# Attention scores from stacked high and low halves in two passes, and the normalisation placed behind the next maximum, in a two-layer diffusion backbone

## The chip, the cores and the metric

The kernel runs on one core of one Trainium2 chip. The metric is the device time in microseconds (us). A core has five engines that run side by side and wait for one another by semaphores: TensorE (PE in the profile, its weight loads PEld), VectorE (DVE), ScalarE (ACT), GpSimd (POOL) and SyncE (SP, which issues most of the loads). Each engine works through its own instructions in the order in which the program emits them.

## What is computed

The reference is a two-layer backbone over 256 latent tokens and 256 context tokens of width 1024. Each layer projects the normalised tokens into a Fourier part, a pooling part, queries, keys, values and gates, mixes them in three branches, and then retrieves experts. The part that the change touches is the attention of one layer:

```python
q = apply_axial_rope(rmsnorm(q, q_norm[l]), ang_row, ang_col)     # 8 heads of 64
k = apply_axial_rope(rmsnorm(k, k_norm[l]), ang_row, ang_col)     # 2 key heads, 4 query heads each
kc = rmsnorm(kc, k_norm[l])
...
s = jnp.einsum('bqhgd,bkhd->bhgqk', q, k).astype(jnp.float32) * (HEAD_DIM ** -0.5)
p = jax.nn.softmax(s, axis=-1).astype(v.dtype)
return jnp.einsum('bhgqk,bkhd->bqhgd', p, v)
```

Latent queries (blocks 0 and 1 of 128 rows) read all 512 keys; context queries (blocks 2 and 3) read the 256 context keys, and only layer 0 has them.

## The kernel before

The order of the work on each engine is the order of the source (a manual schedule). Most large products are three passes over a high and a low half of both operands, kept in the type `fp32r` (helper `mm3`, lines 282 to 284; `split_to`, lines 287 and 289, makes the halves: ACT copies the high one, then DVE or POOL subtracts for the low one). The scores, the transposes against an identity and the products of probabilities and values are exact f32; the trace shows each such f32 call as two PE records ("x2").

`mixer(l, nrm, last)` runs once per layer. It makes `P` (queries and others, 4 blocks of 128 tokens in layer 0, `nq` = 2 in layer 1) and `KV` (keys in its first 128 columns). `rot` normalises and rotates them on DVE. Then come the Fourier and pooling branches, and then the attention:

- **The filler.** `fill()` computes gate projections (units `fills`) as a generator; one `next(filler)` emits six `fp32r` matmuls (L282 to L284, tile `gate`). Eight such steps are emitted ahead of the attention and 24 inside its loop. With the first steps of a unit POOL gets the two subtractions of 1024 columns for the next unit (L289).
- **The preparation (L645 to L653).** Four transposes of the keys (L647), copied to `kT` by ACT; then for each of four pairs of heads `nq` transposes of the queries (L652), copied to `qT`. A pair lies in one tile as two halves of 64 partitions. That is 20 transposes in layer 0 and 12 in layer 1. It is all emitted before the first score.
- **The loop (L710 to L721).** It has N items (head pair, query block, head of the pair): 32 in layer 0, of which 16 have 512 keys and 16 have 256, and 16 of 512 keys in layer 1, so 32 calls of 512 columns and 16 of 256 in all. Round n emits on each engine: `stage_norm(n-1)` (DVE: reciprocal L678, scaling L679), `stage_scores(n)` (PE: one score call L667 with 64 partitions; DVE: maximum L670, L671; ACT: exponential L673), the filler's share, `stage_T(n-2)` (PE transposes L685, ACT copy L687) and `stage_pv(n-3)` (PE products L700 into `ya`). In layer 0 the filler's 24 steps fall into 24 of the 32 rounds, in layer 1 every round has one or two.

Then the remaining gates, the projections of the branches, the output projection (`wout`) and the expert stage follow.

Of the kernel before, what the change touches and what calls it, by code (L numbers as in the profile page):

```python
# [10 lines left out]
F32 = mybir.dt.float32  # L11
F32R = mybir.dt.float32r
F16 = mybir.dt.float16
U32 = mybir.dt.uint32
AF = mybir.ActivationFunctionType
OP = mybir.AluOpType
# [44 lines left out]
def kernel(ctx_: ExitStack, tc: tile.TileContext, I, C, out):  # L61
    nc = tc.nc
# [29 lines left out]
    def b16(shape, dt=F32, name="b16"):  # L92
        return b16_p.tile(shape, dt, tag="b16", name=name)

    def b8(shape, dt=F32, name="b8"):
        return b8_p.tile(shape, dt, tag="b8", name=name)

    def b4(shape, dt=F32, name="b4"):
        return b4_p.tile(shape, dt, tag="b4", name=name)
# [4 lines left out]
    def psum(shape=(128, 512), dt=F32, name="ps"):  # L104
        return banks["ps"].tile(list(shape), dt, tag="ps", name=name)
# [4 lines left out]
    def dram(ap_src, off, dims):  # L110
        return bass.AP(tensor=ap_src.tensor, offset=ap_src.offset + off, ap=dims)
# [3 lines left out]
    ident = perm_p.tile([128, 128], F32, name="ident")  # L115
# [175 lines left out]
    def small(shape, dt=F32, name="small", bufs=None):  # L291
        return sm_p.tile(shape, dt, tag=name, name=name, bufs=bufs) if bufs else sm_p.tile(shape, dt, tag=name, name=name)
# [21 lines left out]
    p = psum()  # L314
# [76 lines left out]
    def ffn_rows(l):  # L391

        rows = small([40, 128], name="mrows", bufs=1)
        frows[l] = rows
        for s in range(2):
            for i, (g, o) in enumerate(((1, 1024), (2, 0))):
                r0 = 16 * s + 8 * i
                load(out=rows[r0:r0 + 8].rearrange("k (b j) -> k b j", b=4),
                     in_=md[l, g][s:s + 1, o:o + 1024].rearrange("a (b k j) -> (a k) b j", b=4, k=8))
        load(out=rows[32:40].rearrange("k (b j) -> k b j", b=4),  # L400
             in_=dram(I["norm_ffn"], l * D, [[32, 8], [256, 4], [1, 32]]))
# [78 lines left out]
    def mixer(l, nrm, last):  # L480
        nq = 2 if last else 4
        nt = nq * 128
        gains = b4([128, 640], name="gains")
        load(out=gains[:, :512].rearrange("p (h d) -> p h d", d=HD),
             in_=dram(I["q_norm"], l * HD, [[0, 128], [0, 8], [1, HD]]))
        load(out=gains[:, 512:].rearrange("p (h d) -> p h d", d=HD),
             in_=dram(I["k_norm"], l * HD, [[0, 128], [0, 2], [1, HD]]))
# [10 lines left out]
        P = b16([128, 4, 1024], name="P")  # L498
        KV = b4([128, 4, 256], name="KV")
# [59 lines left out]
                nc.vector.tensor_tensor(out=v, in0=v, in1=rope[:, b, 0:1, :].to_broadcast([128, nh, HD]), op=OP.mult)  # L559
                nc.vector.tensor_tensor(out=src, in0=src, in1=t, op=OP.add)  # L560

        kT = b4([128, 512], name="kT")
        qT = b8([128, 4, nt], name="qT")
        for b in range(4):
            rot(b, KV[:, b, :128], 8, 2)
            if b < nq:
# [14 lines left out]
        for s in range(nq // 2):  # L581
            for c in range(2):
                ps = psum()
                for k in range(2):
                    nc.tensor.matmul(ps, lhsT=P[:, 2 * s + k, c * 128:(c + 1) * 128], rhs=dft[:, k, :],
                                     start=k == 0, stop=k == 1)
                nc.scalar.activation(pt[:, s, c, :], ps, AF.Copy)
        for c in range(2):
            ps = psum()
            for s in range(nq // 2):  # L590
                for q in range(2):
                    nc.tensor.matmul(ps[:, s * 256:(s + 1) * 256], lhsT=bd[:, q, :],
                                     rhs=pt[:, s, c, q * 256:(q + 1) * 256], start=q == 0, stop=q == 1)
# [4 lines left out]
        for c in range(2):  # L598
            ps = psum()
            for s in range(nq // 2):  # L600
                for g in range(2):
                    ch = 256 + c * 128 + g * 64
                    for k in range(2):
                        nc.tensor.matmul(ps[64 * g:64 * g + 64, s * 256:(s + 1) * 256],
                                         lhsT=P[:, 2 * s + k, ch:ch + 64], rhs=band[:, 2 * c + g, k, :],
                                         start=k == 0, stop=k == 1)
            nc.scalar.activation(pp[:, c, :], ps[:, :nt], AF.Copy)
        S.presplit()
        for c in range(2):
            ps = psum()  # L610
            nc.tensor.matmul(ps[:, :nt], lhsT=pw[:, c, :], rhs=pp[:, c, :], start=True, stop=True)
            t = b4([128, nt], name="pt")
# [29 lines left out]
        filler = fill()  # L642
        for _ in range(8):
            next(filler)
        ps = psum()  # L645
        for b in range(4):
            nc.tensor.transpose(ps[:, b * 128:(b + 1) * 128], KV[:, b, :128], ident)  # L647
        nc.scalar.activation(kT, ps, AF.Copy)
        for j in range(4):
            ps = psum()  # L650
            for b in range(nq):
                nc.tensor.transpose(ps[:, b * 128:(b + 1) * 128], P[:, b, 512 + j * 128:640 + j * 128], ident)  # L652
            nc.scalar.activation(qT[:, j, :], ps[:, :nt], AF.Copy)  # L653

        items = [(hc, b, e) for hc in range(4) for b in range(nq) for e in range(2)]
        st = {}
# [2 lines left out]
        def stage_scores(n):  # L659
            hc, b, e = items[n]  # L660
            h = 2 * hc + e
            v, j = divmod(h, 4)
            kb = (0, 4) if b < 2 else (2, 4)
            nk = (kb[1] - kb[0]) * 128
            ps = psum()
            s = slice(64 * v, 64 * v + 64)
            nc.tensor.matmul(ps[:, :nk], lhsT=qT[s, j, b * 128:(b + 1) * 128], rhs=kT[s, kb[0] * 128:kb[1] * 128],  # L667
                             start=True, stop=True)
            mx = small([128, 3], name="mx", bufs=6)
            nc.vector.tensor_reduce(out=mx[:, 0:1], in_=ps[:, :nk], op=OP.max, axis=AX)  # L670
            nc.vector.tensor_scalar(mx[:, 0:1], mx[:, 0:1], -0.125, None, op0=OP.mult)  # L671
            pm = ring[:, n % 4, :]
            nc.scalar.activation(pm[:, :nk], ps[:, :nk], AF.Exp, bias=mx[:, 0:1], scale=0.125, accum_out=mx[:, 1:2])  # L673
            st[n] = (pm, mx, kb, nk)

        def stage_norm(n):
            pm, mx, kb, nk = st[n]
            nc.vector.reciprocal(out=mx[:, 2:3], in_=mx[:, 1:2])  # L678
            nc.vector.tensor_scalar(pm[:, :nk], pm[:, :nk], mx[:, 2:3], None, op0=OP.mult)  # L679

        def stage_T(n):
            pm, mx, kb, nk = st[n]
            ps = psum()
            for q in range(nk // 128):
                nc.tensor.transpose(ps[:, q * 128:(q + 1) * 128], pm[:, q * 128:(q + 1) * 128], ident)  # L685
            pT = ring[:, 4 + n % 4, :]
            nc.scalar.activation(pT[:, :nk], ps[:, :nk], AF.Copy)  # L687
            st[n] = (pT, kb)
# [3 lines left out]
        def stage_pv(n):  # L692
            hc, b, e = items[n]
            v = (2 * hc + e) // 4
            pT, kb = st.pop(n)
            if b == 0 and e == 0:
                ya[hc] = psum(name="ya")
            for q in range(kb[0], kb[1]):
                o = (q - kb[0]) * 128
                nc.tensor.matmul(ya[hc][64 * e:64 * e + 64, b * 128:(b + 1) * 128],  # L700
                                 lhsT=KV[:, q, 128 + 64 * v:192 + 64 * v], rhs=pT[:, o:o + 128],
                                 start=q == kb[0], stop=q == kb[1] - 1)
            if b == nq - 1 and e == 1:
                split_to(yh[:, 4 + hc, :], yl[:, 4 + hc, :], ya.pop(hc)[:, :nt])

        N = len(items)
        filled = 0
        if l:
            ffn_rows(l)
        for n in range(N + 3):  # L710
            if 0 <= n - 1 < N:
                stage_norm(n - 1)
            if n < N:
                stage_scores(n)
            while filled < min(24 * (n + 1) // N, 24):
                next(filler, None)
                filled += 1
            if 0 <= n - 2 < N:
                stage_T(n - 2)
            if n >= 3:  # L720
                stage_pv(n - 3)  # L721
# [9 lines left out]
        for n, u in enumerate(rest):  # L731
# [22 lines left out]
            for c in range(2):  # L754
                w = slice(c * 128, (c + 1) * 128)
                for i, (k0, k1) in enumerate(br):
                    ps = psum()
# [435 lines left out]
    for l in range(DEPTH):  # L1193
        last = l == DEPTH - 1
        nb = 2 if last else 4
        mg = mixer(l, nrm, last)
        ffn_cols(l)

        def keys():
            kT = b8([128, 16, 128], name="keysT")  # L1200
            for q in range(4):
                ps = psum()
                for a in range(4):
                    nc.tensor.transpose(ps[:, a * 128:(a + 1) * 128], kr[:, 4 * q + a, :], ident)
                nc.scalar.activation(kT[:, 4 * q:4 * q + 4, :], ps.rearrange("p (a n) -> p a n", a=4), AF.Copy)
            return kT

        X = b16([128, nb, D], name="X")
        for b in range(nb):
            if l == 0:  # L1210
                src = I["x"][0, b * 128:(b + 1) * 128, :] if b < 2 else I["ctx"][0, (b - 2) * 128:(b - 1) * 128, :]
            else:
                src = xs[b]
# [27 lines left out]
        if nb == 4:  # L1241
# [12 lines left out]
            kT = keys()  # L1254
# [6 lines left out]
        else:  # L1261
# [10 lines left out]
            kT = keys()  # L1272
# [68 lines left out]
```

## Time and profile before

| | |
|---|---|
| median of three runs | 3029.86 us (3025.63 to 3040.64) |
| the profiled execution | 3029.89 us |
| its span, first to last instruction | 3028.1 us |
| mean granted TensorE clock | 0.963 of full speed |
| busy: PE, PEld, DVE, ACT, POOL | 2761.7, 2414.4, 2151.0, 1290.1, 1243.0 us |

The busy times are sums over the whole span; a PE record's end is modelled, and records of matmuls overlap, so the distance from one start to the next tells what a matmul takes. The attention of layer 0 lies at about 135 to 241 us of the span, that of layer 1 at about 1968 to 2030 us.

### The profile page before, as it was taken

What the parts mean: (1) busy time and instruction counts of PE and PEld (TensorE: products, weight loads), DVE (VectorE), ACT (ScalarE), POOL (GpSimd) and SP (SyncE); (2) the same over time, 40 slices, a digit from 0 to 9 for tenths busy, and PEclk for the clock granted to TensorE, in tenths of its full rate; (3) what the DMA queues carried; (4) which work ended last, traced back from release to release, by engine and by line L of the source; (5) the groups of instructions that cost most, each with busy time, mean ns of one, the idle gap of its engine ahead of it and who ended that gap; (6) DMA issues with size and microseconds to landing.
All of it is one profiled execution on the core that took longest, in us unless ns stands there. A gap on an engine that the chain in (4) does not pass through costs nothing.

```text
span 3028.1 us, 42396 instructions
## 1 busy us (share of the span) xinstructions
PE 2761.7 (91%) x16484; PEld 2414.4 (80%) x16484; DVE 2151.0 (71%) x3292; ACT 1290.1 (43%) x1955; POOL 1243.0 (41%) x634
## 2 busy tenths in 40 slices
PE   6999998999898888999998889799887998899999
PEld 4767786798888777987776777679887988888887
DVE  3444253599999999577776877646797889466666
ACT  3443222233334666332332223454544777544443
POOL 0110002234357898455665555020578767620000
PEclk8999999999999999999999999899999999999999
DMA  6215655768887797989999888426778899987874
GB/s 226 85 41 200 247 178 170 182 161 231 214 226 228 245 269 234 291 321 364 358 369 371 326 336 297 134 71 201 158 173 189 199 239 227 220 283 292 310 288 184
DMA packets 365577, 706.97 MB, mean 233 GB/s; under 512 B 25424, under 2 KB 265456, under 8 KB 351296
## 3 DMA queue, kind: packets, MB, share of 16 engines
q1 hardware_dynamic: 271104, 491.38, 54.3%
q0 software_dynamic: 36864, 134.23, 12.5%
q10 hardware_dynamic: 57408, 78.65, 7.5%
q8 instruction: 129, 2.11, 0.3%
q14 instruction: 72, 0.59, 0.1%
HBM read 619.18 MB, written 85.00 MB: 233 GB/s over the span
## 4 chain that ended last, share of the span: by engine, by line
PE 24%; DMA 16%; DVE 10%; issue 6%; ACT 4%; POOL 2%; SPq 0%; ACTq 0%; DVEq 0%; POOLq 0%
PE acc L1164 14%; DMA picked<-in_peer_v_dram,picks 5%; DMA raw<-in_peer_u_dram 4%; DMA G<-stg 3%; PE ps L284 2%; PE ps L282 2%; PE ps L283 2%; DVE UT L1001 2%; ACT stg L924 1%; DMA H<-Hg 1%; POOL picked L937 1%; DMA picked<-in_peer_u_dram,picks 1%; DVE af L1089 1%; DMA raw<-in_peer_v_dram 1%; DVE hl L1016 1%
## 5 line engine op out<-in xcount | busy, mean ns | idle before, releaser
L1164 PE MATMUL acc<-hl,A 128*128 128x512 f32 x3840 | 890.1, 394 | 40.6 <-ACT A L287 39.1
L1164 PEld LDWEIGHTS acc<-hl,A 128*128 128x128 f32 x3840 | 728.4, 190 | 201.8 <-ACT A L287 45.3
L1016 POOL TENSOR_TENSOR hl<-UT,hl 128x1024 fp32r<-128x1024 f32 x192 | 508.9, 2669 | 396.6 <-ACT hl L1008 388.2
L289 POOL TENSOR_TENSOR hl<-raw,hl 128x1024 fp32r<-128x1024 f32 x112 | 271.1, 2431 | 631.7 <-ACT hl L287 501.2
L284 PE MATMUL ps<-hTh,hl 128*128 128x384 f32 (+2 forms) x1168 | 410.6, 352 | 65.7 <-DVE hl L1016 65.4
L287 ACT ACTIVATE hl<-raw 128x1024 fp32r<-128x1024 f32 x388 | 387.5, 1047 | 91.1 <-DMA raw<-in_peer_wq_dram 42.6
L289 DVE TENSOR_TENSOR hl<-raw,hl 128x1024 fp32r<-128x1024 f32 x276 | 334.1, 1242 | 119.6 <-ACT hl L287 119.3
L282 PE MATMUL ps<-hTh,hl 128*128 128x384 f32 (+2 forms) x1168 | 410.7, 352 | 3.8 <-ACT stg L924 3.8
L283 PE MATMUL ps<-hTl,hl 128*128 128x384 f32 (+2 forms) x1168 | 407.1, 349 | 3.5 <-POOL hTl L289 3.5
L1001 DVE STREAM_TRANSPOSE UT<-raw 128x2048 f32<-128x2048 f32 x128 | 294.1, 2299 | 116.3 <-DMA raw<-in_peer_u_dram 83.7
L282 PE MATMUL ps<-hT,hl 128*128 128x256 f32 x1152 | 337.7, 293 | 18.9 <-ACT Hg L1121 12.1
L284 PE MATMUL ps<-hT,hl 128*128 128x256 f32 x1152 | 335.5, 291 | 18.0 <-POOL hl L1016 18.0
L283 PE MATMUL ps<-hT,hl 128*128 128x256 f32 x1152 | 334.0, 290 | 1.1 <-POOL hT L289 1.1
L1008 ACT ACTIVATE hl<-UT 128x1024 fp32r<-128x1024 f32 x256 | 256.4, 1050 | 177.0 <-DVE UT L1001 149.6
L287 ACT ACTIVATE A<-af 128x768 fp32r<-128x768 f32 (+1 forms) x128 | 94.5, 739 | 526.9 <-DVE af L1089 348.8
L284 PEld LDWEIGHTS ps<-hTh,hl 128*128 128x128 f32 x1168 | 229.2, 196 | 81.3 <-DVE hl L1016 76.7
L282 PEld LDWEIGHTS ps<-hT,hl 128*128 128x128 f32 x1152 | 229.8, 199 | 21.5 <-ACT Hg L1121 13.7
L284 PEld LDWEIGHTS ps<-hT,hl 128*128 128x128 f32 x1152 | 229.2, 199 | 21.3 <-POOL hl L1016 21.3
L282 PEld LDWEIGHTS ps<-hTh,hl 128*128 128x128 f32 x1168 | 228.7, 196 | 16.6 <-ACT stg L924 5.2
L283 PEld LDWEIGHTS ps<-hTl,hl 128*128 128x128 f32 x1168 | 229.0, 196 | 8.0 <-POOL hTl L289 3.7
L968 DVE SCALAR_TENSOR_TENSOR sacc<-picked,picks,sacc 128x1024 f32<-128x1024 f32 x127 | 163.2, 1285 | 97.3 <-DMA picked<-in_peer_v_dram,picks 95.2
L283 PEld LDWEIGHTS ps<-hT,hl 128*128 128x128 f32 x1152 | 229.4, 199 | 1.6 <-POOL hT L289 1.6
(247 smaller groups left out, 4714.2 us busy)
## 6 DMA issues: line engine op xcount, KB each, us to landing
raw<-in_peer_u_dram SPq DMA_DIRECT2D x512, 256.0 KB
raw<-in_peer_v_dram SPq DMA_DIRECT2D x128, 1024.0 KB
raw<-in_ada_w_dram SPq DMA_DIRECT2D x48, 1024.0 KB
G<-stg ACTq DMA_DIRECT2D x20, 2048.0 KB
raw<-in_w_in_dram SPq DMA_DIRECT2D x34, 1024.0 KB
Gq<-G SPq DMA_DIRECT2D x16, 1536.0 KB
H<-Hg ACTq DMA_DIRECT2D x56, 384.0 KB
Hq<-H SPq DMA_DIRECT2D x14, 1536.0 KB
```

Of the source, the lines that this page charges most:

```text
L282: nc.tensor.matmul(ps, lhsT=lh, rhs=rh, start=first, stop=False)
L283: nc.tensor.matmul(ps, lhsT=lh, rhs=rl, start=False, stop=False)
L284: nc.tensor.matmul(ps, lhsT=ll, rhs=rh, start=False, stop=last)
L287: nc.scalar.activation(hi, src, AF.Copy)
L289: eng.tensor_tensor(out=lo, in0=src, in1=hi.bitcast(F32), op=OP.subtract)
L924: nc.scalar.activation(stg[:, :, o:o + 4].rearrange("p i t -> p t i"), pv, AF.Copy, scale=1.0 / GSCALE)
L937: nc.gpsimd.indirect_dma_start(out=SP["buf"][:, k % 4, :], out_offset=None, in_=I[name].rearrange("l e d -> (l e) d"), in_offset=bass.Indi ...
L968: nc.vector.scalar_tensor_tensor(SP["acc"], row, g, SP["acc"], op0=OP.mult, op1=OP.add)
L1001: nc.vector.transpose(t, r)
L1008: nc.scalar.activation(t[:, 0, a], v[:, a], AF.Copy)
L1016: eng.tensor_tensor(out=t[:, 1, a], in0=v[:, a], in1=t[:, 0, a].bitcast(F32), op=OP.subtract)
L1164: nc.tensor.matmul(acc[b][n], lhsT=a4[:, lhs, a, t], rhs=rhs[:, o:o + 512], start=f, stop=e)
```

## The change

The scores keep the high and the low half of a query head stacked on the partitions: partitions 0 to 63 hold the high half and 64 to 127 the low half. The first pass multiplies this by the high half of the keys, which stands twice on the partitions (`kH`), and so gives two of the three products; the second pass has 64 partitions, the high half of the query by the low half of the keys (`kL`). Both are `fp32r`.

For this, each head's 64 columns are put into a tile `twice` two times over by two POOL copies, transposed against the identity (both halves come out with the same values), copied by ACT as the high half, and the lower 64 partitions are overwritten by DVE with the remainder. That is done for two key heads (four blocks each) and eight query heads (`nq` blocks each): ten rounds of `both`, one after the other, all of them emitted before the first score, through one buffer `twice`. The number of transposes goes from 20 to 40 in layer 0 and from 12 to 24 in layer 1. In the loop, `stage_norm(n-1)` is emitted behind `stage_scores(n)`.

```diff
-        kT = b4([128, 512], name="kT")
-        qT = b8([128, 4, nt], name="qT")
         for b in range(4):
             rot(b, KV[:, b, :128], 8, 2)
...
-        ps = psum()
-        for b in range(4):
-            nc.tensor.transpose(ps[:, b * 128:(b + 1) * 128], KV[:, b, :128], ident)
-        nc.scalar.activation(kT, ps, AF.Copy)
-        for j in range(4):
+
+        kH = b4([128, 2, 512], F32R, name="kH")
+        kL = b4([128, 2, 512], F32R, name="kL")
+        qT = [b8([128, 2048 // nt, nt], F32R, name="qT") for _ in range(nt // 256)]
+        twice = b4([128, 4, 2, 64], name="twice")
+
+        def both(src, nblk):
+            t = twice[:, :nblk]
+            for e in range(2):
+                nc.gpsimd.tensor_copy(out=t[:, :, e, :], in_=src)
             ps = psum()
-            for b in range(nq):
-                nc.tensor.transpose(ps[:, b * 128:(b + 1) * 128], P[:, b, 512 + j * 128:640 + j * 128], ident)
-            nc.scalar.activation(qT[:, j, :], ps[:, :nt], AF.Copy)
+            for b in range(nblk):
+                nc.tensor.transpose(ps[:, b * 128:(b + 1) * 128], t[:, b].rearrange("p e d -> p (e d)"), ident)
+            return ps
+
+        for v in range(2):
+            ps = both(KV[:, :, 64 * v:64 * v + 64], 4)
+            nc.scalar.activation(kH[:, v], ps, AF.Copy)
+            nc.vector.tensor_tensor(out=kL[:64, v], in0=ps[:64], in1=kH[:64, v].bitcast(F32), op=OP.subtract)
+        qh = {}
+        for h in range(8):
+            v, j = divmod(h, 4)
+            ps = both(P[:, :nq, 512 + j * 128 + v * 64:576 + j * 128 + v * 64], nq)
+            t = qT[h * nt // 2048][:, h % (2048 // nt), :]
+            nc.scalar.activation(t, ps[:, :nt], AF.Copy)
+            nc.vector.tensor_tensor(out=t[64:], in0=ps[64:, :nt], in1=t[64:].bitcast(F32), op=OP.subtract)
+            qh[h] = t
...
-            s = slice(64 * v, 64 * v + 64)
-            nc.tensor.matmul(ps[:, :nk], lhsT=qT[s, j, b * 128:(b + 1) * 128], rhs=kT[s, kb[0] * 128:kb[1] * 128],
-                             start=True, stop=True)
+            t, ks = slice(b * 128, (b + 1) * 128), slice(kb[0] * 128, kb[1] * 128)
+            nc.tensor.matmul(ps[:, :nk], lhsT=qh[h][:, t], rhs=kH[:, v, ks], start=True, stop=False)
+            nc.tensor.matmul(ps[:, :nk], lhsT=qh[h][:64, t], rhs=kL[:64, v, ks], start=False, stop=True)
...
         for n in range(N + 3):
+            if n < N:
+                stage_scores(n)
             if 0 <= n - 1 < N:
                 stage_norm(n - 1)
-            if n < N:
-                stage_scores(n)
```

## Rows read from the trace of the kernel before

**Rows 1.** Busy time by stretch: start:end, length, engines' busy us (instructions), PEclk, DMA share, GB/s.
```profile
134.95:246.00 111.05, 110.06 (x548) 71.90 (x547) 45.15 (x132) 54.39 (x123) 15.25 (x8) 1.00 0.15 49
1967.88:2030.00 62.12, 61.91 (x382) 44.05 (x380) 27.86 (x67) 32.06 (x69) 17.69 (x8) 1.00 0.23 71
```
**Rows 2.** Timeline of PE, a round of layer 0: start us, us, engine, line, operation.
```profile
202.47 0.70 PE L667 MATMUL ps<-kT,qT 64*128 64x256 f32 x2
203.10 0.50 PE L282 MATMUL gate<-hTh,hl 128*128 128x512 f32 x1
203.43 0.40 PE L283 MATMUL gate<-hTl,hl 128*128 128x512 f32 x1
203.67 0.39 PE L284 MATMUL gate<-hTh,hl 128*128 128x512 f32 x1
```
**Rows 3.** Timeline of PE, a round of layer 1.
```profile
1995.90 1.12 PE L667 MATMUL ps<-kT,qT 64*128 64x512 f32 x2
1996.96 0.38 PE L282 MATMUL gate<-hTh,hl 128*128 128x256 f32 x1
1997.18 0.28 PE L283 MATMUL gate<-hTl,hl 128*128 128x256 f32 x1
1997.30 0.28 PE L284 MATMUL gate<-hTh,hl 128*128 128x256 f32 x1
```
**Rows 4.** Timeline of PE, the Fourier products of layer 0.
```profile
107.36 7.03 PE L585 MATMUL ps<-raw,P 128*128 128x512 f32 x16
114.23 3.62 PE L592 MATMUL ps<-p,raw 128*128 128x256 f32 x16
```
**Rows 5.** Timeline of PE, the preparation of layer 0 and the first score.
```profile
134.95 0.60 PE L647 MATMUL ps<-ident,KV 128*128 128x128 f32 x4
...
137.23 1.98 PE L667 MATMUL ps<-kT,qT 64*128 64x512 f32 x4
```
**Rows 6.** Timeline of all engines, the preparation of layer 1.
```profile
1967.88 0.60 PE L647 MATMUL ps<-ident,KV 128*128 128x128 f32 x4
...
1968.57 0.60 ACT L648 ACTIVATE kT<-ps 128x512 f32<-128x512 f32 x1 [0.91 <-PE ps L647]
...
1969.50 1.12 PE L667 MATMUL ps<-kT,qT 64*128 64x512 f32 x2
```
**Rows 7.** Timeline of POOL, around the preparation of each layer.
```profile
129.88 4.75 POOL L289 TENSOR_TENSOR hl<-raw,hl 128x1024 fp32r<-128x1024 f32 x2 [72.83 <-ACT hl L287]
...
1966.52 4.71 POOL L289 TENSOR_TENSOR hl<-raw,hl 128x1024 fp32r<-128x1024 f32 x2 [42.17 <-ACT hl L287]
```
**Rows 8.** POOL's groups over the span: count, busy us, mean ns, idle before.
```profile
L289 POOL TENSOR_TENSOR hl<-raw,hl 128x1024 fp32r<-128x1024 f32 x112 | 271.1, 2431 | 631.7 <-ACT hl L287 501.2 <-DVE nr L305 110.4 <-issue 19.4
...
L289 POOL TENSOR_TENSOR hTl<-hTf,hTh 128x512 fp32r<-128x512 f32 x12 | 15.7, 1310 | 93.0 <-ACT hTh L287 93.0
L327 POOL MEMSET adab<- 128x512 f32 x6 | 3.1, 526 | 86.9 <-DVE store L762 78.2 <-PE ps L1053 8.4 <-POOLq L1326 0.3
...
L492 POOL MEMSET pr<- 128x256 f32 x2 | 0.6, 312 | 0.0
```
**Rows 9.** Timeline, a PE matmul that waits for a POOL subtraction.
```profile
41.61 1.27 POOL L289 TENSOR_TENSOR hTl<-hTf,hTh 128x512 fp32r<-128x512 f32 x1 [40.09 <-ACT hTh L287]
...
42.93 0.58 PE L284 MATMUL ps<-hl,hTl 128*128 128x256 f32 x1
```
**Rows 10.** Busy time by stretch, two stretches with gaps on PE.
```profile
18.00:21.00 3.00, 1.50 (x12) 0.20 (x8) 0.00 (x0) 0.00 (x0) 0.00 (x0) 1.00 1.02 393
...
2042.00:2046.00 4.00, 2.07 (x9) 1.86 (x10) 3.19 (x4) 4.00 (x7) 0.00 (x0) 0.79 0.01 2
```
**Rows 11.** Timeline of PE at the lower clock.
```profile
33.00 1.12 PE L370 MATMUL ps<-ident,adab 128*128 128x128 f32 x4 [0.87 <-DVE adab L340]
...
2044.44 0.58 PE L284 MATMUL gate<-hTh,hl 128*128 128x256 f32 x1 [0.76 <-DVE hl L289]
...
2047.79 0.28 PE L284 MATMUL gate<-hTh,hl 128*128 128x256 f32 x1
```

## The prediction

> **What bounds the kernel now.** I read the page first and saw PE busy for 91% of the span; then the stretches of the two attentions, because only they are touched. There PE is busy for 110.06 of 111.05 us and for 61.91 of 62.12 us at full clock [rows 1], while DVE and ACT stand at 41 to 52% and the DMA engines at 0.15 to 0.23. So both stretches last as long as PE's own instruction stream: a microsecond of PE work removed there is a microsecond gained, and a microsecond in which PE has to wait for another engine is lost. Nothing behind them takes the difference back: the transfers wait for buffers that PE's use sets free, so a later or earlier PE shifts them with it. Then I read the PE timeline for the price of a score call, and POOL's timeline and groups, because POOL has no part in the preparation now and gets twenty copies per layer.
>
> **The scores: what is saved.** From one start to the next, a 512-column score takes 1996.96 - 1995.90 = 1.06 us [rows 3] and a 256-column one 203.10 - 202.47 = 0.63 us [rows 2]. The first fp32r matmul behind it is 0.10 late as well: 0.33 us to the next start where the following one takes 0.24 [rows 2], 0.22 against 0.12 [rows 3]. An fp32r matmul takes 0.23 for 512 and 0.12 for 256 columns, so two passes are 0.46 and 0.24. The step from f32 to fp32r now lies ahead of the score instead of behind it, so its 0.10 stays: 0.56 and 0.34 against 1.16 and 0.73, which saves 0.60 and 0.39. That is the best case. The worst: eight f32 calls of 512 columns without a change of operands take (114.23 - 107.36)/8 = 0.86 each [rows 4], so 0.20 of the 1.06 belongs to the change of shape around the call, a weight load that nothing hides. If the new pair pays that too (128 partitions, then 64, then 128 again), it saves 0.40 and 0.19. With 32 wide and 16 narrow calls: best 32 x 0.60 + 16 x 0.39 = 25.4 us, worst 15.8, and I take the middle, 20.6, since no row shows a 64-partition fp32r pass. In the 8 rounds of layer 0 without a filler step the old call had no fp32r matmul behind it and no 0.10, which takes off 0.8: **19.8 us saved** (15.0 to 24.6).
>
> **The preparation: what is added.** Before, it is bare PE work: 20 transposes in 137.23 - 134.95 = 2.28 us in layer 0 (0.114 each) [rows 5], and 1.62 us in layer 1 [rows 6]. After, each of the ten rounds is a chain through one buffer: two POOL copies, the transposes, and only then may POOL write `twice` again. ACT's copy and DVE's subtraction of a round run beside the next round. PE has nothing else to do meanwhile: all filler steps ahead are done and the scores are emitted behind, so every microsecond of the chain is a PE stall.
>
> Links of the chain: POOL to PE 0.05 us (POOL ends at 41.61 + 1.27 = 42.88, PE starts at 42.93) [rows 9]; four transposes 0.60 from the first start to the modelled end, two of them 0.60 - 2 x 0.114 = 0.37; PE to the next engine 0.09 (1967.88 + 0.60 = 1968.48, ACT starts at 1968.57) [rows 6], which I use for PE to POOL.
>
> The copies: a copy has 256 columns where there are four blocks and 128 where there are two (the query rounds of layer 1). No POOL copy is in the trace. From below, a memset of 256 columns takes 0.312, and by the slope between 256 and 512 (0.526) one of 128 takes 0.205. From above, a two-input subtraction takes 1.310 for 512 and 2.431 for 1024 columns, so by that slope 0.75 for 256 and 0.47 for 128 [rows 8]. A copy reads one stream and a memset none, a subtraction two; I take a fifth of the way up, 0.40 and 0.26. [...]
>
> Layer 0: POOL is in its subtractions until 129.88 + 4.75 = 134.63 [rows 7], just before PE arrives at 134.95, so nothing more is lost there. The first transposes start at 134.63 + 0.80 + 0.05 = 135.48, a round is 0.80 + 0.05 + 0.60 + 0.09 = 1.54, and the tenth set ends its issue at 135.48 + 9 x 1.54 + 0.46 = 149.80 instead of 137.23: 12.6 us lost. Layer 1: the copies queue behind subtractions that last until 1966.52 + 4.71 = 1971.23 [rows 7], 3.35 us after PE has arrived at 1967.88. First set at 1972.08, second at 1973.62, third (first of two blocks) at 1974.88, then seven rounds of 0.52 + 0.05 + 0.37 + 0.09 = 1.03, end at 1982.32 instead of 1969.50: 12.8 us lost. Together **25.4 us** (22.4 by the memset, 37.2 by the subtraction). This holds the doubled transposes too, which alone would be 32 x 0.114 = 3.6.
>
> **The clock.** At 2042 to 2046 us PE is busy for 2.07 of 4 us and the granted clock falls to the lower level for part of it [rows 10]; fifteen filler matmuls then take 3.35 us (2044.44 to 2047.79) [rows 11] where 15 x 0.12 = 1.8 is the full-clock price, so 1.5 are lost behind a fall. Four transposes at the lower clock last 1.12 instead of 0.60 [rows 11]. In layer 1 PE stands still for 4.2 us and is then busy for a third of the time, so I expect the fall: 2 x 0.52 + 8 x 0.3 + 1.5 = **5.0 us**. In layer 0 it is busy for 0.60 of each 1.54 us without a long pause; at 18 to 21 us it was busy for half of the time and kept the full clock [rows 10]. I take no fall there; if it comes, it is 10 x 0.52 + 1.5 = 6.7.
>
> **The rest.** `stage_norm(n-1)` behind `stage_scores(n)`: on DVE the two operations that wait for the exponential no longer stand ahead of the maximum, which waits for PE. Behind them on DVE wait the next maximum and, through it, ACT's exponential; the probabilities that they scale are needed by PE one round later. PE hardly waits for this chain now (0.99 us in layer 0, 0.21 in layer 1 [rows 1]), so the swap has nothing to gain: 0. It would cost where a maximum is late; with rounds shorter by some 0.6 us the waits at the loop's start may double in each layer, so I add **1.0 us** (0 to 2). ACT and DVE get ten operations each in a stretch where they idle: 0. The later place of `qT` and the three tiles for one `kT`: 0, since the buffers that they take belong to work that ended before PE reached the preparation; were one still held, the first copy would wait for it.
>
> **Sum:** 25.4 + 5.0 + 1.0 - 19.8 = +11.6 us on 3029.9 (the profiled execution, 1.8 us above its span and equal to the median within 0.1): **3041.5 us**. All costs low: 22.4 - 24.6 = -2.2, 3027.7. All high: 37.2 + 5.0 + 6.7 + 2 - 15.0 = +35.9, 3065.8.
>
> **Rivals.** A measurement tells 0.5%, here 15.1 us, from no change.
> - *The preparation is cheap.* Copies at the memset's price, full clock throughout, passes that hide their weight loads: -2 to +3 us, 3028 to 3033. For it: one input stream only. Against: the 3.35 us behind POOL's queue in layer 1 remain and invite the lower clock.
> - *The clock falls in layer 0 too* (the other side: slower). The same sum plus 6.7 is +18.3, 3048.2. For it: twelve microseconds at 39% busy are a longer lean stretch than any that kept the clock in these rows. It decides from 3.5 us on top of my sum, seven of ten rounds at the lower clock.
> - *The copies cost what two inputs cost:* +23.4, 3053.3; or the two-pass score hides no weight load at all, which ends near +16. The second would be a change that doesn't do what it says.
> - *Faster by over 15 us* needs a preparation of under 8 us more in both layers together, which no bound here allows; only an effect that I can't see would do it.
>
> **Chances.** My sum 0.45 (3034 to 3049, a quarter of it beyond 3045), the cheap preparation 0.15, the clock in layer 0 0.20, dear copies or passes 0.12, faster by something unseen 0.08. So faster 0.08, same 0.15 + 0.33 + 0.06 = 0.54 (0.06 from the slower cases where other terms come out low), slower 0.38. The range leaves out the fastest case and the upper half of the dear one: 3026 to 3058.
>
> **What would show it.** The page of the changed kernel should show POOL copies of 0.3 to 0.5 us, PE waiting for POOL for some 10 us in each preparation, layer 1's first copy right behind the subtractions, and score pairs of 0.56 to 0.76 us from start to start. In the stretch from the preparation to the last product, layer 0 should be about as long as before and layer 1 longer by some 10 us. I am wrong if the copies run ahead of the transposes, if PE keeps its clock in layer 1, or if PE waits inside the loop, which would mean that DVE's new order, not PE, sets the pace.

## The result and the profile after

| | before | after |
|---|---|---|
| median of four runs each | 3035.25 us (3025.63 to 3045.19) | 3069.27 us (3058.36 to 3072.87) |
| after over before | | 1.010, 95% interval 1.0071 to 1.0129 |
| profiled execution: time, span | 3029.89, 3028.1 us | 3072.87, 3071.1 us |
| mean granted clock | 0.963 | 0.95 |

The change makes the kernel slower by 1.0%, about 30 us. The forecast was 3041.5 with a range of 3026 to 3058: the sign of its sum (+11.6) was right, the size was not, and of its outcomes it held no measurable change the likeliest (0.54 against 0.38 for slower).

The page of the kernel after hides the loss: PE is busy for 2785.4 us, the same 91% as before, in a longer span. So I measure each attention by two marks on ACT that both kernels have: the start of a copy of `P` ahead of it (in layer 0 the first of all these copies, in layer 1 the last) and the start of a store of the sigmoid behind it (in layer 0 the first, in layer 1 the last). These are the answers for the two lines, first of before, then of after (count, shortest, median and longest ns, start of the first, which is in layer 0, and of the last, which is in layer 1):

```profile
L519 ACT ACTIVATE P<-ps x24: 360/384/387, 64.4 to 1952.4; 128x256 f32<-128x256 f32 x24
L746 ACT ACTIVATE store<-store x8: 615/836/1062, 243.2 to 2052.0; 128x1024 f32<-128x1024 f32 x4, 128x512 f32<-128x512 f32 x4
L746 ACT ACT_TABLE_LOAD  x2: 1283/1283/1283, 241.9 to 2030.9; - x2
```

```profile
L519 ACT ACTIVATE P<-ps x24: 362/383/385, 63.4 to 1974.3; 128x256 f32<-128x256 f32 x24
L762 ACT ACTIVATE store<-store x8: 615/838/1062, 256.3 to 2087.8; 128x1024 f32<-128x1024 f32 x4, 128x512 f32<-128x512 f32 x4
L762 ACT ACT_TABLE_LOAD  x2: 1283/1283/1283, 255.0 to 2066.6; - x2
```

From the first L519 to the first store is layer 0: 178.8 before, 192.9 after. From the last L519 to the last store is layer 1: 99.6 before, 113.5 after. Together +28.0 us, which agrees with the loss that the runs time (about 30). The two profiled spans differ by 43.0; the other 15.0 lie in stretches that the change doesn't touch, and runs of one kernel differ by as much. The sum of the two stretches is called *the stretch* below.

**Preparation, layer 0.** All engines of the kernel after, around its first two rounds:

```profile
133.81 0.39 PE L284 MATMUL gate<-hTh,hl 128*128 128x512 f32 x1
134.45 0.66 PE L655 MATMUL ps<-ident,twice 128*128 128x128 f32 x4 [0.25 <-POOL twice L652]
...
135.24 0.74 POOL L652 COPY twice<-KV 128x256 f32<-128x256 f32 x2 [0.84 <-PE ps L655]
136.03 0.66 PE L655 MATMUL ps<-ident,twice 128*128 128x128 f32 x4 [0.93 <-POOL twice L652]
...
139.25 1.12 PE L655 MATMUL ps<-ident,twice 128*128 128x128 f32 x4 [0.93 <-POOL twice L652]
141.30 1.12 PE L655 MATMUL ps<-ident,twice 128*128 128x128 f32 x4 [0.93 <-POOL twice L652]
...
152.30 0.78 PE L683 MATMUL ps<-kH,qT 128*128 128x512 f32 x1
```

The chain is as forecast: copies, transposes, copies again, each naming the other as its releaser. A round takes 136.03 - 134.45 = 1.58 us (forecast 1.54). But from 139.25 the four transposes last 1.12 instead of 0.66 and a round 2.05. PE comes to the preparation at 133.81 + 0.23 = 134.04 and scores from 152.30: 18.26 us, against 2.28 before [rows 5]. In windows of 2 us (columns as in [rows 1]) the granted clock falls from the upper to the lower level (1.00 to 0.50 of full speed) while PE is busy for about half of each window:

```profile
136.00:138.00 2.00, 1.05 (x8) 0.81 (x8) 1.09 (x2) 0.60 (x1) 0.74 (x2) 1.00 0.89 302
138.00:140.00 2.00, 1.07 (x7) 0.74 (x5) 0.73 (x2) 0.60 (x1) 0.74 (x2) 0.52 0.13 45
...
152.00:156.00 4.00, 4.00 (x10) 2.16 (x9) 2.23 (x4) 1.60 (x2) 0.00 (x0) 0.50 0.00 0
```

The last row is behind the preparation: PE is busy throughout and still has the lower clock, 0.50.

**Preparation, layer 1.** Timeline of POOL and PE:

```profile
1988.33 4.68 POOL L289 TENSOR_TENSOR hl<-raw,hl 128x1024 fp32r<-128x1024 f32 x2 [42.53 <-ACT hl L287]
1992.95 0.74 POOL L652 COPY twice<-KV 128x256 f32<-128x256 f32 x2
1993.74 0.66 PE L655 MATMUL ps<-ident,twice 128*128 128x128 f32 x4 [3.89 <-POOL twice L652]
...
2006.92 0.78 PE L683 MATMUL ps<-kH,qT 128*128 128x512 f32 x1
```

Here too the forecast holds: the first copies stand behind the subtractions in POOL's queue, and PE waits 3.89 us for them. PE comes at 1989.69 and scores from 2006.92: 17.23 us, against 1.62 before [rows 6].

**The scores.** Timeline of PE, full clock, a wide call and the filler behind it, then a narrow call:

```profile
160.76 0.47 PE L683 MATMUL ps<-kH,qT 128*128 128x512 f32 x1
161.17 0.18 PEld L684 LDWEIGHTS ps<-kL,qT 64*128 64x128 f32 x1 [0.24 <-issue]
161.17 0.50 PE L684 MATMUL ps<-kL,qT 64*128 64x512 f32 x1
161.60 0.19 PEld L282 LDWEIGHTS gate<-hTh,hl 128*128 128x128 f32 x1 [0.25 <-issue]
161.60 0.50 PE L282 MATMUL gate<-hTh,hl 128*128 128x512 f32 x1
161.94 0.40 PE L283 MATMUL gate<-hTl,hl 128*128 128x512 f32 x1
...
164.65 0.39 PE L683 MATMUL ps<-kH,qT 128*128 128x256 f32 x1
164.96 0.39 PE L684 MATMUL ps<-kL,qT 64*128 64x256 f32 x1
165.28 0.66 PE L701 MATMUL ps<-ident,ring 128*128 128x128 f32 x4
```

This is where the forecast fails. The wide pair takes 161.60 - 160.76 = 0.84 and the matmul behind it is still 0.11 late (0.34 to the next start instead of 0.23): 0.95 against 1.16 before [rows 3]. That is the first pair at full clock; most wide pairs take 0.86. The narrow pair takes 0.31 + 0.32 = 0.63, as the f32 call did [rows 2]. Look at the two weight loads: each begins together with its own matmul, with PEld idle for 0.24 us ahead of it. Among the filler's passes, all of 128 partitions, it is otherwise:

```profile
133.36 0.39 PE L282 MATMUL gate<-hTh,hl 128*128 128x512 f32 x1
133.36 0.19 PEld L283 LDWEIGHTS gate<-hTl,hl 128*128 128x128 f32 x1
133.58 0.39 PE L283 MATMUL gate<-hTl,hl 128*128 128x512 f32 x1
```

There the load for L283 begins with the matmul ahead (133.36), is done by 133.55, and its own matmul starts 0.22 after that one.

### The profile page after: what moved, and what is told of

The parts are those of the page before. It is cut to its first block, busy times and chain, and to the rows that moved or that the text cites. A ratio compares the mean times of both kernels' runs of the same rounds, so it can differ in the third digit from the quotient of the medians.

```text
span 3071.1 us, 42565 instructions
## 1 busy us (share of the span) xinstructions
PE 2785.4 (91%) x16516; PEld 2438.8 (79%) x16516; DVE 2162.1 (70%) x3312; ACT 1296.0 (42%) x1965; POOL 1250.5 (41%) x674
## 4 chain that ended last, share of the span: by engine, by line
PE 23%; DMA 16%; DVE 9%; issue 6%; ACT 4%; POOL 3%; SPq 1%; ACTq 0%; DVEq 0%; POOLq 0%
PE acc L1180 14%; DMA picked<-in_peer_v_dram,picks 5%; DMA raw<-in_peer_u_dram 5%; DMA G<-stg 3%; DVE UT L1017 2%; PE ps L284 2%; PE ps L283 2%; PE ps L282 1%; DMA H<-Hg 1%; ACT stg L940 1%; POOL picked L953 1%; DMA picked<-in_peer_u_dram,picks 1%; POOL hl L289 1%; DVE af L1105 1%; DMA raw<-in_peer_v_dram 1%
## 5 line engine op out<-in xcount | busy, mean ns | idle before, releaser
L283 PE MATMUL ps<-hTl,hl 128*128 128x384 f32 (+2 forms) x1168 | 408.6, 350 | 3.5 <-POOL hTl L289 3.5
L284 PE MATMUL ps<-hT,hl 128*128 128x256 f32 x1152 | 338.5, 294 | 18.3 <-POOL hl L1032 18.2
L283 PE MATMUL ps<-hT,hl 128*128 128x256 f32 x1152 | 336.6, 292 | 1.1 <-POOL hT L289 1.1
L283 PEld LDWEIGHTS ps<-hTl,hl 128*128 128x128 f32 x1168 | 230.4, 197 | 7.9 <-POOL hTl L289 3.7
L283 PEld LDWEIGHTS ps<-hT,hl 128*128 128x128 f32 x1152 | 231.6, 201 | 1.6 <-POOL hT L289 1.6
```

Source lines behind the costliest of these rows:

```text
L283: nc.tensor.matmul(ps, lhsT=lh, rhs=rl, start=False, stop=False)
L284: nc.tensor.matmul(ps, lhsT=ll, rhs=rh, start=False, stop=last)
```

## The experiments

Ratios are to the kernel before, run on the same chip beside each kernel; the stretch is from the profiled execution, against 278.4 us before.

| kernel | ratio, 95% interval | stretch, us |
|---|---|---|
| after | 1.010 (1.0071 to 1.0129) | +28.0 |
| e1: before, swapped order alone | 0.999 (0.997 to 1.0011) | -1.3 |
| e2: after, second pass on 128 partitions | 1.0026 (1.0009 to 1.0044) | +7.7 |
| e3: after, PE kept busy | 1.0075 (1.0051 to 1.0099) | +18.2 |
| e4: after, two buffers `twice` | 1.0035 (1.0017 to 1.0052) | +8.2 |
| e5: e2 and e4 | 0.9984 (0.997 to 0.9999) | -9.6 |
| e6: e2, copies early, rounds among the filler | 0.9951 (0.9933 to 0.9968) | -19.7 |
| e7: e6 with the change's own scores | 0.9986 (0.9972 to 1.0) | -5.0 |
| e8: e6 with the old order | 0.996 (0.9949 to 0.9972) | -14.6 |
| e9: before, three `fp32r` passes on 64 partitions | 1.0002 (0.9985 to 1.0018) | -4.8 |

Stretch and ratio tell the same order; a thousandth of the time is 3.0 us, and the two agree within some 5 us.

**e1, the order alone.** The kernel before, with only the last part of the change:

```diff
         for n in range(N + 3):
+            if n < N:
+                stage_scores(n)
             if 0 <= n - 1 < N:
                 stage_norm(n - 1)
-            if n < N:
-                stage_scores(n)
```

> The kernel before, with nothing of the change but the order in the loop: the normalisation behind the next step's scores. Theory (the preparation and the price of the two passes make all of the +28 us that the two attention stretches show): 0, ratio 0.998 to 1.002, both attention stretches within 1 us of before. Rival (the new order on DVE makes PE wait): a part of the +28 us is here, ratio 1.003 or more, with PE waits for the scaling or for the copy of the transposed probabilities in the loop.

Measured: 0.999, an interval around 1. PE's waits from 100 to 260 us in before (total us, times, longest); e1 has the second line alone, which is not the loop's:

```profile
PE ya L700 <- ACT ring L687: 1.0, 3, 0.6
PE gate L284 <- DVE hl L289: 0.5, 1, 0.5
```

The swap takes away the 1.0 us that PE waited in layer 0's loop, and the stretch is 1.3 us shorter (1.1 in layer 0, 0.2 in layer 1). That is too little for the run times to tell from nothing, and it is a gain. So the loss comes from the rest of the change, the scores and their preparation.

**e2, the second pass on 128 partitions.** `kL` is made twice on the partitions like `kH`, and the second pass multiplies both halves of the query by it. This adds the product of the two low halves, which the change leaves out.

```diff
-  nc.vector.tensor_tensor(out=kL[:64, v], in0=ps[:64], in1=kH[:64, v].bitcast(F32), op=OP.subtract)
+  nc.vector.tensor_tensor(out=kL[:, v], in0=ps, in1=kH[:, v].bitcast(F32), op=OP.subtract)
...
-  nc.tensor.matmul(ps[:, :nk], lhsT=qh[h][:64, t], rhs=kL[:64, v, ks], start=False, stop=True)
+  nc.tensor.matmul(ps[:, :nk], lhsT=qh[h][:, t], rhs=kL[:, v, ks], start=False, stop=True)
```

> The changed kernel, with the second pass on all 128 partitions (low half of the keys on both halves of the partitions, same stationary operand as the first pass; it adds the product of the two low halves, nothing else). Theory (the second pass and what follows it pay about 0.2 us each because a weight load for another number of partitions is not hidden): second pass 0.23 instead of 0.42 for 512 columns and 0.12 instead of 0.31 for 256, 48 calls, 9 to 18 us less than the changed kernel, ratio to before 1.004 to 1.007. Rival (a second pass into the same bank, or the score's place in the stream, costs 0.42 whatever its shape): passes unchanged, ratio 1.009 to 1.011.

Measured: 1.0026, better than expected. The preparation is untouched, and the stretch is 20.3 us shorter than after's (9 to 18 were expected). Timeline of PE, a narrow call with what stands ahead of it, then a wide one:

```profile
162.20 0.60 PE L701 MATMUL ps<-ident,ring 128*128 128x128 f32 x4
162.73 1.09 PE L716 MATMUL ya<-ring,KV 128*64 128x128 f32 x8
163.75 0.19 PEld L683 LDWEIGHTS ps<-kH,qT 128*128 128x128 f32 x1 [0.17 <-issue]
163.75 0.39 PE L683 MATMUL ps<-kH,qT 128*128 128x256 f32 x1
163.97 0.28 PE L684 MATMUL ps<-kL,qT 128*128 128x256 f32 x1
164.09 0.40 PE L282 MATMUL gate<-hTh,hl 128*128 128x512 f32 x1
164.32 0.40 PE L283 MATMUL gate<-hTl,hl 128*128 128x512 f32 x1
...
172.68 0.50 PE L683 MATMUL ps<-kH,qT 128*128 128x512 f32 x1
173.01 0.39 PE L684 MATMUL ps<-kL,qT 128*128 128x512 f32 x1
173.24 0.38 PE L701 MATMUL ps<-ident,ring 128*128 128x128 f32 x2
```

The pairs take 0.33 + 0.23 = 0.56 and 0.22 + 0.12 = 0.34, the forecast's best case to the hundredth, and the filler behind is not late (0.23). The loads are as many as in the kernel after (48 at L684); twice the partitions cost nothing, and the change from 128 partitions to 64 and back costs 0.95 - 0.56 = 0.39 a call. The two passes of e2 share their stationary operand, but the filler's passes, which change it each time, hide their loads too (0.23 from start to start).

The first pass is still 0.10 long (0.33 and 0.22 instead of 0.23 and 0.12). Ahead of it stand the products of probabilities and values, whose stationary operand has 128 partitions but 64 columns (`128*64`), and the first pass's load again begins with its own matmul (163.75), with PEld idle for 0.17 ahead of it. So it is not the partitions alone: in these loops the load is late wherever the stationary operand's shape changes, its partitions or its columns. In the kernel after, from 160 to 255 and from 2014 to 2066 us, the trace shows 175 changes among `128*128`, `128*64` and `64*128`, and at each of them the load begins within 0.01 us of its own matmul. The type does not matter, as e6 will show.

**e3, PE kept busy.** Each round gets two more matmuls (four in layer 1) into a bank that nothing reads; they are added work that only holds PE busy.

```diff
+            junk = psum(name="keep")
+            for i in range(4 if nq == 2 else 2):
+                nc.tensor.matmul(junk[:, :nt], lhsT=hh[:, i, :128], rhs=hh[:, i, :nt], start=True, stop=True)
             return ps
```

> The changed kernel, with two (layer 1: four) extra matmuls behind each of the ten preparation rounds, into a bank that nobody reads, 0.46 us of work in a wait of 0.93. Theory (the rounds stretch from 1.6 to 2.05 us in layer 0 and the first scores run at half speed because the clock falls): the granted clock stays at its upper level, rounds 1.6 and 1.1 us, about 10 us less than the changed kernel, ratio to before 1.005 to 1.008. Rival (the clock is a side effect and the rounds are slow for another reason): same as the changed kernel or slower by the 9 us of extra matmuls, ratio 1.009 to 1.013.

Measured: 1.0075, as expected. Layer 0's preparation, after's window first and e3's below it:

```profile
134.00:152.00 18.00, 9.38 (x39) 6.02 (x39) 6.22 (x9) 5.37 (x9) 7.08 (x20) 0.61 0.18 59
```

```profile
134.00:152.00 18.00, 13.50 (x68) 8.07 (x67) 7.88 (x13) 6.02 (x11) 7.32 (x20) 1.00 0.19 59
```

With PE busy for 13.50 instead of 9.38 of 18 us the clock stays at the upper level, and a kernel with more work is 9.8 us shorter in the stretch: 5.4 in layer 0, 4.4 in layer 1 (where the first rounds, behind the 3.89 us, still have the lower clock: the second's four transposes last 1.12 us). So the lower clock was a cost of its own, and it hit layer 0 too.

**e4, two buffers.** The rounds use two tiles `twice` in turn, so POOL can fill one while PE reads the other.

```diff
-        twice = b4([128, 4, 2, 64], name="twice")
+        twice = [b4([128, 4, 2, 64], name="twice") for _ in range(2)]
+        turn = [0]
...
-            t = twice[:, :nblk]
+            t = twice[turn[0] % 2][:, :nblk]
+            turn[0] += 1
```

> The changed kernel, with two buffers twice used in turn, so that POOL may fill one while PE transposes the other. Theory (the ten rounds are a chain of POOL and PE through the one buffer): a round lasts as long as POOL's two copies, 0.75 to 0.85 us in layer 0 and 0.55 to 0.65 in layer 1, 16 to 21 us less than the changed kernel, ratio to before 1.002 to 1.005. Rival (POOL's copies themselves, or their start behind its queue, are the cost): under 5 us less, ratio 1.008 to 1.011.

Measured: 1.0035, as expected. PE's rounds in layer 0:

```profile
133.56 1.34 PE L657 MATMUL ps<-ident,twice 128*128 128x128 f32 x8 [0.24 <-POOL twice L654]
135.15 1.34 PE L657 MATMUL ps<-ident,twice 128*128 128x128 f32 x8 [0.24 <-POOL twice L654]
```

In layer 0 two rounds take 1.59 us where one took 1.58, and the granted clock stays at 1.00. In layer 1 it still falls behind PE's wait of 3.89 us: from the first score at 1981.66 to 1989.82 PE works at the lower level (filler passes of 256 columns start 0.21 us apart, and 0.12 from 1990.15 on), though none of its rows in that time shows a wait. The stretch is 19.8 us shorter: the one buffer and, in layer 0, what it does to the clock were more than half of what the preparation and the restart behind it cost (36.6 in the table below). What is left is POOL's copying time, still ahead of the scores, its queue in layer 1, and the lower clock there.

**e5, both repairs.** e2's scores with e4's buffers.

> The changed kernel with both repairs: two buffers twice in turn, and the second pass on all 128 partitions. Theory (the two costs stand in different places and add): 19 us by the buffers and 22 by the partitions less than the changed kernel, ratio to before 0.994 to 0.998. Rival (they hide each other, so that the second repair gives little once the first is in): 1.000 to 1.003.

Measured: 0.9984, just above what was expected; the stretch is at -9.6. The two repairs by themselves took 20.3 and 19.8 off it, 40.1, and both together take 28.0 + 9.6 = 37.6. They nearly add up, so they mend separate losses in the main.

**e6, copies early and rounds among the filler.** e2's scores; POOL's copies go into three tiles and are emitted right behind the rotation (six of the ten sets in layer 0, all ten in layer 1), and the eight filler steps are put between the ten rounds. `put(i)` is the two copies of a round, `round_(i)` its transposes, ACT copy and DVE subtraction, and behind them the next of the `late` sets. The core of the edit:

```diff
+        ahead = 6 if nq == 4 else 10
+        for i in range(ahead):
+            put(i)
+        late = list(range(ahead, 10))
...
-        for _ in range(8):
-            next(filler)
+        for i in range(10):
+            round_(i)
+            if i < 8:
+                next(filler)
```

> The second pass on all 128 partitions, and the preparation taken out of PE's way: the first copies are emitted right behind the rotation, into three buffers, and the ten rounds of transposes stand between the eight filler steps. Theory (what is left of the preparation is its transposes, 32 more at 0.114 us, and the scores save 0.60 and 0.39 us a call as in the best case of the prediction): PE never waits for POOL in the preparation, 24.6 - 3.6 = 21 us less than before, ratio 0.991 to 0.995. Rival (the early copies or the rounds between the filler steps cost elsewhere, on ACT, DVE or in the Fourier stage): 0.996 or more.

Measured: 0.9951, at the edge of what was expected and faster than both kernels (-19.7 in the stretch, -21 expected). PE's waits from 100 to 260 us, and the first rounds:

```profile
PE ps L723 <- DVE ring L717: 1.4, 1, 1.4
PE ya L738 <- ACT ring L725: 1.0, 2, 0.6
```

```profile
120.64 0.60 PE L674 MATMUL ps<-ident,twice 128*128 128x128 f32 x4
121.00 0.48 PE L282 MATMUL gate<-hTh,hl 128*128 128x512 f32 x1
121.31 0.40 PE L283 MATMUL gate<-hTl,hl 128*128 128x512 f32 x1
```

No wait for POOL is left. Four transposes and the filler matmul behind them take 0.67 us (120.64 to 121.31), which leaves 0.44 for the transposes, 0.11 each; the round's copies run beside other work. So a step from f32 to `fp32r` between operands of one shape costs nothing. In layer 0 what the loop's start now waits for is the score's own chain (maximum, exponential, scaling), 2.4 us.

**e7, the change's scores in e6.** The two lines of e2 taken back.

> As e6_early, but with the second pass on 64 partitions as in the change. Theory (the change's scores by themselves save 0.2 us on each of 32 wide calls and nothing on the narrow ones, about what the 32 more transposes cost): -2 to -5 us against before, ratio 0.998 to 1.000. Rival (the stall of the preparation was all that was wrong): as e6_early, 0.991 to 0.995.

Measured: 0.9986 with an upper bound of 1.0. With the preparation hidden, the change's own scores are worth next to nothing; 14.7 us of stretch separate them from those on 128 partitions.

**e8, the old order in e6.** The swap of e1 undone in e6.

> As e6_early, but with the normalisation ahead of the next step's scores, as before. Theory (PE sets the pace of the loop, and the order on DVE is free in either kernel): same as e6_early within 0.002. Rival (with rounds of PE shorter by 0.6 us the order begins to matter, which is what it was moved for): 3 us or more longer than e6_early, with PE waits for the scaled probabilities or for the copies behind them.

Measured: 0.996, whose interval overlaps e6's (0.9933 to 0.9968), so the times don't tell the two orders apart. The profile leans to the swap: the stretch is 5.1 us longer, and the wait for the probabilities in layer 0 has grown from 1.0 to 3.8, the longest 2.3. From 100 to 250 us the same transposes (L723) and products (L738) also take 280 and 287 ns in the mean, against 273 and 281 in e6. It is one profiled execution of each.

```profile
PE ya L738 <- ACT ring L725: 3.8, 3, 2.3
```

**e9, 64 partitions alone.** The kernel before, with its scores as three `fp32r` passes, all on 64 partitions, and no doubled tiles. The core of the edit:

```diff
-            nc.tensor.matmul(ps[:, :nk], lhsT=qT[s, j, b * 128:(b + 1) * 128], rhs=kT[s, kb[0] * 128:kb[1] * 128],
-                             start=True, stop=True)
+            t, ks = slice(b * 128, (b + 1) * 128), slice(kb[0] * 128, kb[1] * 128)
+            mm3(ps[:, :nk], qT[0][s, j, t], qT[1][s, j, t], kT[0][s, ks], kT[1][s, ks], True, True)
```

> The kernel before with its preparation and order, but the scores as three fp32r passes on 64 partitions each, high by high, high by low, low by high, with the halves made from the transposes as they come (no copies by POOL, no doubled transposes; ten more subtractions on DVE in the two layers together). Theory (not 64 partitions but the change from one number to another leaves a weight load unhidden): the first pass pays 0.2, the second and third 0.23 or 0.12, a call 0.88 and 0.55 us instead of 1.06 and 0.63, 7 us less than before, ratio 0.996 to 0.999. Rival (every fp32r pass on 64 partitions pays 0.2): 1.26 and 0.93 us, 11 us more than before, ratio 1.002 to 1.005.

Timeline of PE, a wide call:

```profile
160.46 0.50 PE L282 MATMUL ps<-kT,qT 64*128 64x512 f32 x1
160.80 0.39 PE L283 MATMUL ps<-kT,qT 64*128 64x512 f32 x1
161.03 0.39 PE L284 MATMUL ps<-kT,qT 64*128 64x512 f32 x1
161.35 0.44 PE L687 MATMUL ps<-ident,ring 128*128 128x128 f32 x2
```

The middle pass, 64 partitions behind 64, takes 0.23 like one of 128 behind 128; only the first (0.34) and the last (0.32, ahead of 128 partitions) are long. The three take 0.89, and the narrow ones 0.55, as the theory of the switch summed them, though it had put 0.2 on the first pass alone: the first pass is 0.11 long, as e2's first pass of 128 partitions is behind the same products, and 0.09 falls on the last. So 64 partitions cost nothing as such; the step between 64 and 128 does. The whole kernel's time, 1.0002, is no different from before's: the expected gain of some thousandths didn't show. In the profiled execution most of it is there, -4.8 of the stretch, and PE waits 2.5 us for the probabilities in layer 0 where it waited 1.0 before, and 0.9 in layer 1 where it waited for none. That makes up for the rest of the 7 that were expected; the run times neither show nor exclude some 4 us.

## Why the prediction was wrong

Four terms, all in us. The measured ones are from the profiled executions: the preparation from PE's arrival to the first score; the restart is the work at the lower clock behind it against the same work at the upper one (6.62 in layer 0 where e3 takes 3.85 from its first score, 4.96 in layer 1 where the later rows of the same stretch make it 2.79); the last line is the rest of the loop, from the first score to the sigmoid's table load (104.7 to 102.7 in layer 0, 61.4 to 59.7 in layer 1, together -3.7), less the restart.

| term | forecast | measured |
|---|---|---|
| preparation, layer 0 | +12.6 | 18.26 - 2.28 = +16.0 |
| preparation, layer 1, its clock included | 12.8 + 3.5 = +16.3 | 17.23 - 1.62 = +15.6 |
| restart at the lower clock | +1.5 | 2.8 + 2.2 = +5.0 |
| scores and waits in the loops | 1.0 - 19.8 = -18.8 | -3.7 - 5.0 = -8.7 |
| sum | +11.6 | +27.9 |

**The step that failed is the score saving** of 19.8. Its best case, 0.56 and 0.34, is what e2 measures. Its worst case let the pair pay the unhidden weight load of the old call once, 0.20. It pays about twice that: once on the way from 128 partitions to 64, once on the way back, 0.39 together. That leaves 1.16 - 0.95 = 0.21 for a wide call and nothing for a narrow one: 32 x 0.21 = 6.7 (6.6 summed over all calls of e3, which keeps the upper clock in both loops), below the worst case (15.0). I had written "128 partitions, then 64, then 128 again" and priced it as one change. Of the other 2.0 of the -8.7, 1.3 is the swap's (e1); 0.7 I have not traced.

One term of the best case was right by luck. The 0.10 that I took for the step from f32 to `fp32r` has nothing to do with the type: f32 transposes and an `fp32r` matmul of the same shape follow each other at no cost (e6), and in the kernel after the filler is 0.11 late behind an `fp32r` pass of 64 partitions. In [rows 2] and [rows 3] it was the second half of the way back from 64 partitions to 128. It stays ahead of the new pair only because the products that mostly stand there have 64 columns (e2). Read that way, those rows put 0.10 of the price of 64 partitions outside the call, on top of the 0.20 inside it that the worst case charged.

**The second miss is the clock in layer 0**, which I left to a rival with a chance of 0.20. It fell there, after about three rounds at half load. The preparation then cost 16.0 - 12.6 = 3.4 more and the restart 2.8, together 6.2, near the 6.7 that the rival was given; 5.4 of it is the clock's, which e3 gets back by keeping PE busy. That PE had kept the upper clock at 18 to 21 us at about the same busy share [rows 10] did not carry over to this stretch, and no run here shows why. So the two rivals, "the clock falls in layer 0" and "the two-pass score hides no weight load", happened at once, and the second was priced at half of its cost. With 6.7 for 19.8 and 6.2 more for the clock the same sum would have been +30.9, near the 28.0 measured. The forecast's own signs show both misses: the pairs take 0.84 and not 0.56 to 0.76, and layer 0 is 14.1 us longer where it was to stay about as long as before.

**Right:** the chain through one buffer, with rounds of 1.58 against 1.54; the 4.05 us (1993.74 - 1989.69) that PE stands in layer 1 behind POOL's queue (forecast 4.20); the lower clock in layer 1; no wait inside the loop from the swap (it takes 1.0 us of waits away, where 1.0 had been added for them). ACT, DVE and the tiles' later places were put at 0, and the four terms leave nothing for them. The copies, for which no row stood, were taken at 0.40 and 0.26. Their groups:

```profile
L652 POOL COPY twice<-P 128x256 f32<-128x256 f32 x16 | 5.9, 401 | 9.6 <-PE ps L655 8.7 <-POOL twice L652 0.8
L652 POOL COPY twice<-P 128x128 f32<-128x128 f32 x16 | 4.2, 294 | 7.0 <-PE ps L655 7.0
```

A copy of 128 more columns takes 401 - 294 = 107 ns more, and so does a memset by its slope, (526 - 312)/2 [rows 8]; the two-input subtraction takes (2431 - 1310)/4 = 280. So a copy's columns go with the memset's here, and a subtraction's cost 2.6 times as much. A pair back to back takes 0.74, so the pair was sized well.

The weight loads themselves are the same size: 0.18 us for 64 partitions and 0.19 for 128 (161.17, 161.60); only their place differs. So a load's time does not go with the partitions here. A load for a 128-partition pass behind another one is hidden in these runs: the filler row above (load at 133.36 beside a matmul of 128 partitions, next start 0.22 later) and e2's second pass (0.23) show it.

**Open:** why the load is late only where the stationary operand's shape changes (the runs give its price and place, not the mechanism inside PE); whether the swap is worth the 5 us in the shorter rounds that e8's profile hints at; whether the 4.8 us of e9's profiled execution are there in its other runs; and what exactly makes the clock fall and come back: e3 shows that more work on PE keeps it in layer 0, no more, and in e4's layer 1 it stayed low for some 8 us of work without a wait.

## What to carry to other kernels

Price a shorter product with its neighbours: count each place where consecutive matmuls change the number of partitions or of columns of the stationary operand, on the way in and on the way out (here 0.39 us a call for both), and where a second pass would need half of the rows, give it all of them (e2: 20.3 us of the stretch). A preparation that goes through another engine belongs into time that is already filled, with a buffer for each round in flight; left bare on PE it cost its chain here, then the lower clock, then the restart behind it, 36.6 us in both layers. Where two rivals rest on separate mechanisms, add them up for the upper end of the range.

## What was not expected of the hardware

- A change between 64 and 128 partitions from one `fp32r` matmul to the next leaves the weight load unhidden: about 0.2 us each way (0.39 a call for both, e2 against after), with 512 and with 256 moving columns alike. 64 behind 64 takes the same 0.23 for 512 columns as 128 behind 128 (e9). A change between 64 and 128 columns of the stationary operand does the same (e2: 0.10 on the first pass, its load begun with its own matmul), and a change between f32 and `fp32r` at one shape does not (e6: 0.67 us for four transposes and the matmul behind them, 4 x 0.11 + 0.23).
- The granted clock fell in the third round of layer 0, with PE busy for 1.05 of the 2 us ahead of it, and in both layers of the kernel after it stayed at the lower level (0.50) for 5 to 6 us of full work behind the preparation. Added matmuls that nobody reads made the kernel 9.8 us shorter in the stretch (e3).
